# An encoder layer on one core: the mixer's TensorE work and loads in source order, probabilities turned one step later

## The chip, the cores and the metric

The kernel runs on one core of one Trainium2 chip. The metric is the device time of one execution in microseconds (us); lower is better. The engines are named as in the profile: PE (TensorE; PEld is its weight load), DVE (VectorE), ACT (ScalarE), POOL (GpSimd) and SP (SyncE). SP only issues DMA transfers; POOL issues a few on a queue of its own.

## The reference

One layer on x of 512 positions by 1024 channels, all in float32:

```python
x = x + 0.5 * swiglu(rms_norm(x, ffn1_norm), ffn1_w_gate, ffn1_w_up, ffn1_w_down)   # D_FF = 2752
h = rms_norm(x, mix_norm)
u = h @ w_in                                  # [ fourier 512 | q 8x64 | k 2x64 | v 2x64 ]
f_out = fourier_mixer(u[..., :512], fnet_w, fnet_b)   # real(fft2) per group of 128, then a 128x128 map
a_out = gqa_attention(q, k, v, q_norm, k_norm)        # per-head rms_norm, 2-D rotary, softmax, 4 q heads a kv head
x = x + jnp.concatenate([f_out, a_out], axis=-1) @ w_out
x = x + 0.5 * swiglu(rms_norm(x, ffn2_norm), ffn2_w_gate, ffn2_w_up, ffn2_w_down)
return rms_norm(x, final_norm)
```

## The kernel before

Everything is kept transposed: x is eight tiles of 128 channels by 512 positions (`x[0]` to `x[7]`). Each operand of a product is split into a high part and a low remainder, and `product` (L100 to L103) makes three products of them: high by high, high by low, low by high. So a weight tile that comes from memory is used in three steps: SP issues the load into one of three `raw` buffers (`raw_tile`, L87), ACT writes the high part into a ring slot (L96; for `f0` and `f1` DVE does, L94), and DVE writes the low part into another (`lows`, L72). There are six such slots for weights in the mixer, that is three pairs; a pair is free when the products of the tile before are done.

The kernel has three stages: FFN1, the mixer, FFN2. Both FFNs are built inside `in_order()`, which fixes the order of PE's and SP's instructions to that of the source:

```python
def in_order():
    return tc.manual_schedule(engines={mybir.EngineType.PE, mybir.EngineType.SP})
```

In the mixer, before the change, a scheduler of the build sets the order on all engines from a simulated timeline. The last products of FFN1 are called `dn` in the profile (its down projection).

The mixer begins with two memory pools; their tiles lie where FFN1's tiles were. `cos` and `sin` (L557, L559; 256 KB each) are loaded by SP into them, `chan`, `pos` (1 MB) and `odd` by POOL (L842). Then come, in the source's order:

- `project(c, name)` for k, q0, v, q1, q2, q3: a load `raw_in`, the split, and eight steps of `product` with 512 columns into one PSUM bank.
- `rope`: a square, the rotation with cos and sin. For q1, q2 and q3 (`SWAP_DMA`) ACT writes `own_q` (L587), and SP copies its four blocks of 32 partitions in another order to `sw_q` (four DMAs, L591); then DVE multiplies and adds (L596, L599, L600).
- `heads`: sums of squares per head with PE (`pq`, L607), then small DVE operations (L612 to L614, L618) and a power on POOL (L615).
- `keys`: a broadcast `kw` on DVE (L638) is turned by PE (`kp`, L644) and scales the keys, which are split into `ks`. `query` makes `qa` and `qb` (L627, L629). `value_stacks` turns the values (`vp`) into `vst`.

From there on two streams are woven together. `attend(n)` does for step n the scores of one pair of heads and one block of 128 queries (`s`, two products; then a maximum on DVE, L781, L782, and the exponential on ACT, L784, into `e`), the turn of an earlier step (`pt`, four transposes, L790; then ACT's copy `ph`, L793, and DVE's low part `pl`), and the values of a still earlier one (`o`, L809 and L810). A step's index counts 4 head pairs by 2 key heads by 4 blocks, 32 in all. `fill` is a list of the other work with a cost for each: the rest of q1 to q3, the Fourier projections (`f`, L700 to L702), their weight map (`map`), the transform over positions (`dft`) and over channels (`pc`, `psn`). Ahead of each step, entries of `fill` are run until their share of the total cost is reached, a tenth ahead (`FILL_LEAD`).

After the last step, w_out runs over eight output blocks d. Each sums eight parts k: 0 to 3 are the Fourier groups, 4 to 7 the head pairs; the bank is added to `x[d]`, and the norm of FFN2 begins.

Of the kernel before, what the change touches and what calls it, by code (L numbers as in the profile page):

```python
# [16 lines left out]
KD = D // P  # L17
# [7 lines left out]
FILL_LEAD = 0.1  # L25
# [18 lines left out]
def encoder(ctx, tc, A, out):  # L44
# [8 lines left out]
    def bank(name):  # L53
        return pp.tile([P, S], F32, tag="bank", name=name)
# [9 lines left out]
    def in_order():  # L64
        return tc.manual_schedule(engines={mybir.EngineType.PE, mybir.EngineType.SP})

    def run(steps):
        for _, f, a in steps:
            f(*a)

    def lows(lo, src, hi):
        nc.vector.tensor_tensor(out=lo, in0=src, in1=asf(hi), op=ALU.subtract)  # L72
# [17 lines left out]
    def weights(src, name, n=KD, raw=None):  # L90
        raw = raw or raw_tile(src, name, n)
        hi, lo = weight_slots()
        if name in HI_DVE:
            nc.vector.tensor_copy(hi[:, :n, :], raw[:, :n, :])  # L94
        else:
            nc.scalar.copy(hi[:, :n, :], raw[:, :n, :])  # L96
        lows(lo[:, :n, :], raw[:, :n, :], hi[:, :n, :])
        return hi, lo

    def product(ps, whi, wlo, mhi, mlo, first, last):  # L100
        nc.tensor.matmul(ps, whi, mhi, start=first, stop=False)  # L101
        nc.tensor.matmul(ps, whi, mlo, start=False, stop=False)  # L102
        nc.tensor.matmul(ps, wlo, mhi, start=False, stop=last)  # L103

    class Norm:
# [41 lines left out]
        def sum(self, ps, c, parts, first=True, last=True):  # L147
            for i, p in enumerate(parts):
                nc.tensor.matmul(
                    ps[:, 2 * c : 2 * c + 2], p[:, c * P : (c + 1) * P], ones,  # L150
                    start=first and i == 0, stop=last and i == len(parts) - 1,
                )
# [391 lines left out]


    n2 = Norm(2)
    with tc.tile_pool(name="mix", bufs=1) as mp, tc.tile_pool(name="mixt", bufs=1) as mt:

        more = mp.tile([P, 2, KD * P], F32R, name="more")
        more = [more[:, i, :] for i in range(2)]  # L550
# [167 lines left out]
        mh, ml = ([e[g // 2][g % 2].rearrange("p a b -> p (a b)") for g in range(4)] for e in (eh, el))  # L718
# [52 lines left out]
        def scores(t, b, c):  # L771
            if b == 0 and c == 0:
                zs[t] = tp.tile([P, 4, 2], F32, tag="z", bufs=2, name=f"z{t}")
            q = (qa, qb)[b][t]
            cs = slice(c * P, (c + 1) * P)
            ps = bank(f"s{t}{b}{c}")
            nc.tensor.matmul(ps, q[:, cs], kst[b][0], start=True, stop=False)
            nc.tensor.matmul(ps, q[:, cs], kst[b][1], start=False, stop=True)
            f = sc[:, c, 2 + 2 * t + b : 3 + 2 * t + b]
            mx = tp.tile([P, 1], F32, tag="mx", bufs=8, name=f"mx{t}{b}{c}")  # L780
            nc.vector.tensor_reduce(out=mx, in_=ps, axis=AX.X, op=ALU.max, negate=True)  # L781
            nc.vector.tensor_tensor(out=mx, in0=mx, in1=f, op=ALU.mult)  # L782
            e = temp(f"e{t}{b}{c}")
            nc.scalar.activation(e, ps, AF.Exp, bias=mx, scale=f, accum_out=zs[t][:, c, b : b + 1])  # L784
            prob[t, b, c] = e

        def turn(t, b, kc):
            pt = bank(f"pt{t}{b}{kc}")
            for c in range(4):
                nc.tensor.transpose(pt[:, c * P : (c + 1) * P], prob[t, b, c][:, kc * P : (kc + 1) * P], ident)  # L790
            ph = mt.tile([P, S], F32R, tag="ph", bufs=3, name=f"ph{t}{b}{kc}")
            pl = mt.tile([P, S], F32R, tag="pl", bufs=3, name=f"pl{t}{b}{kc}")
            nc.scalar.copy(ph, pt)  # L793
            lows(pl, pt, ph)
            parts[t, b, kc] = ph, pl
            if b == 1 and kc == 0:

                zw = tp.tile([P, 4, 2, HD], F32, tag="wide", bufs=1, name=f"zw{t}")
                nc.vector.reciprocal(zs[t], zs[t])
                nc.gpsimd.tensor_copy(zw, zs[t].unsqueeze(3).to_broadcast([P, 4, 2, HD]))  # L800
                zs[t] = zw

        def values(t, b, kc):
            if kc == 0:
                outs[t, b] = bank(f"o{t}{b}")
            po = outs[t, b]
            ph, pl = parts[t, b, kc]
            w = vst[:, b, kc].rearrange("p a e -> p (a e)")
            nc.tensor.matmul(po, w, ph, start=kc == 0, stop=False)  # L809
            nc.tensor.matmul(po, w, pl, start=False, stop=kc == 3)  # L810
            if kc == 3:
                own = slice(b * HD, (b + 1) * HD)
                if b == 0:
                    pair[t] = tp.tile([P, S], F32, tag="u", name=f"oo{t}")
                o = pair[t]
                nc.scalar.copy(o[own], po[HD:P])
                nc.vector.tensor_tensor(out=o[own], in0=po[0:HD], in1=o[own], op=ALU.add)
                if b == 1:
                    zp = bank(f"zp{t}")
                    for c in range(4):  # L820
                        nc.tensor.transpose(
                            zp[:, c * P : (c + 1) * P], zs[t][:, c].rearrange("p a b -> p (a b)"), ident
                        )
                    nc.vector.tensor_tensor(out=o, in0=zp, in1=o, op=ALU.mult)
                    nc.scalar.copy(qa[t], o)
                    lows(qb[t], o, qa[t])
# [31 lines left out]
        fill = []  # L858
# [34 lines left out]
        def attend(n):  # L893
            def at(m):
                return m // 8, m // 4 % 2, m % 4

            if n < 32:
                scores(*at(n))
            if 4 <= n < 36:
                turn(*at(n - 4))  # L900
            if n >= 6:
                values(*at(n - 6))

        whole = sum(c for c, _, _ in fill)
        done = 0.0
        for n in range(38):
            while fill and done < whole * (FILL_LEAD + (1 - FILL_LEAD) * n / 38):
                done += fill[0][0]
                run([fill.pop(0)])
            attend(n)  # L910
        run(fill)

        mh, ml = mh + [qa[t] for t in range(4)], ml + [qb[t] for t in range(4)]
        for d in range(KD):
            whi, wlo = weights(A["wo"][d], f"o{d}")
            ps = bank(f"out{d}")
            for k in range(KD):
                product(ps, whi[:, k, :], wlo[:, k, :], mh[k], ml[k], k == 0, k == KD - 1)
            nc.vector.tensor_tensor(out=x[d], in0=ps, in1=x[d], op=ALU.add)
            n2.add(d)  # L920

# [5 lines left out]
    ready = (3, 4, 5)  # L927
# [158 lines left out]
```

## Time and profile before

| | us |
|---|---|
| median of 3 runs | 882.02 (881.49 to 883.07) |
| the profiled execution, its own time | 882.0 |
| its span in the profile | 880.1 |
| PE busy | 863.1 |
| DVE busy | 640.4 |
| ACT busy | 451.0 |
| first product of the mixer (`k`) starts at | 353.17 |
| first product of w_out (`out`) starts at | 478.28 |

Times inside the span are counted from its start. A line of a group or of the timeline has the source line (L101), engine, operation, output and inputs by their names in the program, shape, count and duration; `SPq` is SP issuing a DMA. In a table by stage the columns are the stretch, its length, the busy time and count of PE, PEld, DVE, ACT and POOL, the granted clock of PE, the DMA engines' busy share and GB/s. "A <- B: t, n, m" in a list of waits says that A waited for B, t us in total, n times, m at the longest. A matmul's end is modelled, so from start to start is the measure of what one costs in a stream.

### The profile page before, as it was taken

The page shows a single profiled execution, that of the slowest core. Times are in us where ns is not written, and L with a number is a line of the kernel's source. Part 1 is how long each engine was busy: PE and PEld are TensorE (multiplying, and loading weights), DVE is VectorE, ACT ScalarE, POOL GpSimd, SP SyncE. Part 2 cuts the span into 40 slices and gives each one's busy share as a digit, 9 for nine tenths or more (in the row PEclk, how much of TensorE's full clock was granted, in tenths as well). Part 3 has the DMA queues.
Part 4 walks back from the last instruction along what each step waited for, and adds up shares of the span by engine and source line. Part 5 has one row for each costly group of instructions (what it writes and reads, how often), then busy time and mean ns, then how long its engine had stood idle before and what let it go on. Part 6 is the DMA issues. An engine that isn't in the chain of part 4 may idle for free.

```text
span 880.1 us, 13432 instructions
## 1 busy us (share of the span) xinstructions
PE 863.1 (98%) x5334; PEld 766.7 (87%) x5334; DVE 640.4 (73%) x1003; ACT 451.0 (51%) x746; POOL 24.7 (3%) x32
## 2 busy tenths in 40 slices
PE   8999999999999999999999999999999999999995
PEld 5888999889989988888888888889998999889985
DVE  7798788459757837699888558977975688469444
ACT  7454466226525634677775436535652365327432
POOL 0000000000000000211000000000000000000002
PEclk9999999999999999999999999999999999999998
DMA  7324232333243113521110223242224232322212
GB/s 245 112 67 164 98 118 86 99 116 104 69 141 114 55 36 108 204 83 37 50 48 25 94 67 127 75 141 97 108 79 140 88 119 69 105 110 85 73 36 96
DMA packets 29150, 85.55 MB, mean 97 GB/s; under 512 B 3488, under 2 KB 6560, under 8 KB 28960
## 3 DMA queue, kind: packets, MB, share of 16 engines
q1 hardware_dynamic: 28560, 83.37, 28.1%
q0 software_dynamic: 384, 1.32, 0.5%
q8 instruction: 41, 0.67, 0.3%
q14 instruction: 21, 0.17, 0.1%
q10 hardware_dynamic: 144, 0.02, 0.0%
HBM read 81.81 MB, written 2.10 MB: 95 GB/s over the span
## 4 chain that ended last, share of the span: by engine, by line
PE 56%; issue 39%; DVE 2%; ACT 2%; DMA 1%; POOL 0%; SPq 0%; POOLq 0%; ACTq 0%; DVEq 0%
PE r L304 10%; PE q L304 5%; PE dn L103 4%; PE dn L101 4%; PE dn L102 4%; PE p L304 3%; PE gu L103 2%; PE gu L102 2%; PE gu L101 2%; PE out L101 2%; PE out L103 2%; PE out L102 2%; PE pt L790 1%; PE q L101 1%; PE q L102 1%
## 5 line engine op out<-in xcount | busy, mean ns | idle before, releaser
L304 PE MATMUL r<-rt,ring 128*128 128x256 f32 x1584 | 207.2, 283 | 0.0
L304 PEld LDWEIGHTS r<-rt,ring 128*128 128x128 f32 x1584 | 196.1, 188 | 2.4
L101 PE MATMUL dn<-at,ring 128*128 128x512 f32 x324 | 128.0, 395 | 0.8 <-ACT ring L96 0.8
L103 PE MATMUL dn<-at,ring 128*128 128x512 f32 x324 | 127.9, 395 | 0.3 <-DVE ring L72 0.3
L102 PE MATMUL dn<-at,ring 128*128 128x512 f32 x324 | 127.9, 395 | 0.0
L390 DVE SCALAR_TENSOR_TENSOR xt<-dn,xt 128x512 f32<-128x512 f32 x62 | 42.8, 690 | 89.4 <-PE dn L103 89.4
L304 PE MATMUL q<-rt,ring 128*128 128x256 f32 x792 | 104.8, 282 | 0.0
L96 ACT CAST ring<-raw_dn 128x768 fp32r<-128x768 f32 (+3 forms) x64 | 48.1, 754 | 108.2 <-PE dn L102 89.8
L304 PEld LDWEIGHTS q<-rt,ring 128*128 128x128 f32 x792 | 98.7, 188 | 0.0
L72 DVE TENSOR_TENSOR ring<-s,ring 128x1024 fp32r<-128x1024 f32 x66 | 80.3, 1220 | 16.7 <-PE r L304 9.7
L265 ACT CAST ring<-s 128x1024 fp32r<-128x1024 f32 x66 | 69.3, 1050 | 37.4 <-PE r L304 19.2
L103 PEld LDWEIGHTS dn<-at,ring 128*128 128x128 f32 x324 | 61.0, 188 | 15.2 <-DVE ring L72 0.7
L101 PEld LDWEIGHTS dn<-at,ring 128*128 128x128 f32 x324 | 60.9, 188 | 14.8 <-ACT ring L96 1.0
L102 PEld LDWEIGHTS dn<-at,ring 128*128 128x128 f32 x324 | 60.9, 188 | 13.9
L72 DVE TENSOR_TENSOR ring<-raw_dn,ring 128x768 fp32r<-128x768 f32 (+3 forms) x64 | 54.5, 854 | 11.3 <-ACT ring L96 8.9
L304 PE MATMUL p<-rt,ring 128*128 128x256 f32 x396 | 52.4, 282 | 0.0
L72 DVE TENSOR_TENSOR ring<-raw_g,ring 128x1024 fp32r<-128x1024 f32 x33 | 40.4, 1223 | 15.5 <-PE p L304 10.9
L304 PEld LDWEIGHTS p<-rt,ring 128*128 128x128 f32 x396 | 49.3, 188 | 0.0
L265 ACT CAST ring<-raw_g 128x1024 fp32r<-128x1024 f32 x33 | 34.6, 1049 | 22.9 <-PE r L304 9.9
L101 PE MATMUL gu<-ring 128*128 128x512 f32 x112 | 44.1, 394 | 0.9 <-ACT ring L527 0.9
L102 PE MATMUL gu<-ring 128*128 128x512 f32 x112 | 43.9, 392 | 0.0
L103 PE MATMUL gu<-ring 128*128 128x512 f32 x104 | 41.1, 395 | 0.8 <-DVE ring L72 0.7
(308 smaller groups left out, 1514.0 us busy)
## 6 DMA issues: line engine op xcount, KB each, us to landing
raw_g<-in_wgu SPq DMA_DIRECT2D x33, 512.0 KB, 3.7
raw_u<-in_wgu SPq DMA_DIRECT2D x33, 512.0 KB, 4.3
raw_dn<-in_wd SPq DMA_DIRECT2D x40, 384.0 KB, 3.0
raw_gu<-in_wgu SPq DMA_DIRECT2D x16, 512.0 KB, 3.6
raw_o<-in_wo SPq DMA_DIRECT2D x8, 512.0 KB, 3.5
raw_in<-in_wins SPq DMA_DIRECT2D x6, 512.0 KB, 4.1
raw_dn<-in_wd SPq DMA_DIRECT2D x8, 320.0 KB, 2.9
raw_dn<-in_wd SPq DMA_DIRECT2D x8, 256.0 KB, 2.6
```

The costliest lines, as they stand in the source:

```text
L72: nc.vector.tensor_tensor(out=lo, in0=src, in1=asf(hi), op=ALU.subtract)
L96: nc.scalar.copy(hi[:, :n, :], raw[:, :n, :])
L101: nc.tensor.matmul(ps, whi, mhi, start=first, stop=False)
L102: nc.tensor.matmul(ps, whi, mlo, start=False, stop=False)
L103: nc.tensor.matmul(ps, wlo, mhi, start=False, stop=last)
L265: nc.scalar.copy(hi, src)
L304: nc.tensor.matmul(ps, a[:, ks], b[:, i], start=first and i == 0 and o == 0, stop=i == KH - 1 and o == 2, skip_group_check=not first,)
L390: nc.vector.scalar_tensor_tensor(out=x[d][:, t], in0=ps[:, t], scalar=0.5, in1=x[d][:, t], op0=ALU.mult, op1=ALU.add)
L790: nc.tensor.transpose(pt[:, c * P : (c + 1) * P], prob[t, b, c][:, kc * P : (kc + 1) * P], ident)
```

## The change

The mixer too is built inside `in_order()`. The probabilities of step n are turned at step n+5 (before: n+4) and multiplied with the values at step n+7 (before: n+6), so there are 39 steps. In w_out the parts are summed in the order 0, 1, 2, 4, 5, 6, 3, 7 (before: 0 to 7). No computation is added or left out.

```diff
-    with tc.tile_pool(name="mix", bufs=1) as mp, tc.tile_pool(name="mixt", bufs=1) as mt:
+    with in_order(), tc.tile_pool(name="mix", bufs=1) as mp, tc.tile_pool(name="mixt", bufs=1) as mt:
...
             if n < 32:
                 scores(*at(n))
-            if 4 <= n < 36:
-                turn(*at(n - 4))
-            if n >= 6:
-                values(*at(n - 6))
+            if 5 <= n < 37:
+                turn(*at(n - 5))
+            if n >= 7:
+                values(*at(n - 7))
 
         whole = sum(c for c, _, _ in fill)
         done = 0.0
-        for n in range(38):
-            while fill and done < whole * (FILL_LEAD + (1 - FILL_LEAD) * n / 38):
+        for n in range(39):
+            while fill and done < whole * (FILL_LEAD + (1 - FILL_LEAD) * n / 39):
...
+        ready = 0, 1, 2, 4, 5, 6, 3, 7
         for d in range(KD):
             whi, wlo = weights(A["wo"][d], f"o{d}")
             ps = bank(f"out{d}")
-            for k in range(KD):
-                product(ps, whi[:, k, :], wlo[:, k, :], mh[k], ml[k], k == 0, k == KD - 1)
+            for k in ready:
+                product(ps, whi[:, k, :], wlo[:, k, :], mh[k], ml[k], k == ready[0], k == ready[-1])
```

DVE, ACT and POOL stay with the scheduler. The source has the loads of cos and sin ahead of the first `project`.

## The prediction

> **What bounds the kernel now.** I read first the page's busy times and chain, then a table by stage of the mixer (353 to 527 us), then who waits for whom there, then SP's queue at the mixer's entrance, since SP's order is what the change rewrites.
>
> ```profile
> PE 863.1 (98%) x5334; PEld 766.7 (87%) x5334; DVE 640.4 (73%) x1003; ACT 451.0 (51%) x746; POOL 24.7 (3%) x32
> ```
>
> TensorE (PE) is the bound: 17 us without a product in 880.1. What it can gain in the mixer is its idle time there. The stage table (PE busy is the second number):
>
> ```profile
> 353.00:380.00 27.00, 27.00 (x138) 22.63 (x137) 19.76 (x34) 17.63 (x26) 5.82 (x6) 1.00 0.51 179
> 380.00:400.00 20.00, 20.00 (x106) 16.69 (x105) 19.20 (x41) 16.18 (x32) 2.78 (x2) 1.00 0.24 70
> 400.00:410.00 10.00, 8.75 (x59) 7.44 (x58) 9.87 (x24) 7.60 (x17) 2.24 (x2) 1.00 0.24 73
> ...
> 430.00:440.00 10.00, 9.09 (x66) 8.20 (x65) 8.00 (x17) 6.62 (x15) 0.00 (x0) 1.00 0.30 105
> ...
> 450.00:460.00 10.00, 9.51 (x61) 8.01 (x60) 8.92 (x17) 8.50 (x16) 0.00 (x0) 1.00 0.32 105
> 460.00:470.00 10.00, 9.60 (x65) 8.00 (x64) 8.81 (x19) 6.90 (x17) 0.23 (x1) 1.00 0.15 54
> 470.00:480.00 10.00, 9.54 (x64) 8.41 (x63) 8.82 (x20) 6.36 (x14) 0.39 (x1) 1.00 0.01 2
> 480.00:527.00 47.00, 47.00 (x205) 37.90 (x204) 26.70 (x37) 19.23 (x27) 0.00 (x0) 1.00 0.21 69
> ```
>
> PE is full up to 400 and in w_out. Idle shows in five rows: 1.25 + 0.91 + 0.49 + 0.40 + 0.46 = 3.5 us. The modelled tail of a product hides part of each stall; from start to start along PE's timeline, less the usual pitch (0.231 us for 512 columns, 0.119 for 256, 0.109 for a transpose), the loss from 353.2 to 478.3 is 5.7 us, 4.4 of it in five stalls (404, 437, 459, 466, 471). So 5.7 us is all that any order of the attention stage can bring. DVE is at 19.2 of 20 in the second row: it has no room there.
>
> Now the entrance. SP's timeline, SP's waits, and PE's timeline at the same time:
>
> ```profile
> 334.12 17.50 SPq L87 DMA_DIRECT2D raw_in<-in_wins  x4
> 353.36 0.33 SPq L557 DMA_DIRECT2D cos<-in_cos  x1
> 353.74 0.43 SPq L559 DMA_DIRECT2D sin<-in_sin  x1
> 355.52 1.46 SPq L87 DMA_DIRECT2D raw_in<-in_wins  x2
> ```
>
> ```profile
> SPq L557 <- PE dn L103: 1.7, 1, 1.7
> ```
>
> ```profile
> 352.94 0.39 PE L103 MATMUL dn<-at,ring 128*128 128x512 f32 x1
> 352.94 0.19 PEld L101 LDWEIGHTS k<-ring 128*128 128x128 f32 x1
> 353.17 0.40 PE L101 MATMUL k<-ring 128*128 128x512 f32 x1
> ```
>
> The first four weight tiles of the mixer are issued from 334.12 on, under FFN1's last products. The load of cos waits 1.7 us for a product of FFN1's `dn` (its tile lies in FFN1's memory) and goes out at 353.36, after the last one. PE passes from `dn` to `k` with no gap, because `k`'s weights are there.
>
> **The change, part by part.** The built program of the changed kernel has SP in source order: cos, sin, and only then raw_in 0, 1, 5, 2, 3. The wait ahead of cos is on the same product as before, the last of `dn`. So all weight loads of the mixer queue behind FFN1's end.
>
> *Opening.* cos at 353.36, sin at 353.74 (0.43), raw_in 0 at about 354.2. How long until it lands? The nearest rows:
>
> ```profile
> DMA to landing us min/median/max: 3.5/4.1/7.4
> ```
>
> ```profile
> q0 software_dynamic: 70, 0.57, 93.1%
> q1 hardware_dynamic: 7, 0.03, 4.8%
> ```
>
> The first is of the six raw_in loads: 3.5 to 4.1 on a quiet queue; the two issued at 355.5 and 356.7 took 7.3 and 7.4. The second pair is the DMA share by queue from 358 to 360: the 1 MB load of pos, which POOL issues at 354.24 on its own queue q0, has the engines nearly alone, and SP's q1 stands. raw_in 0 would be issued 1.3 us before those two, behind cos and sin, beside the same pos. Bounds: 4.1 (358.3) and the landing of the load whose place it takes (362.8); I take 361.9, next to the 7.3 row. Then the cast on ACT (1.05; the first product needs it), then the low part on DVE (1.23; the third product needs it), hops 0.15: third product of `k` at 364.3 instead of 353.63: **+10.7** (7.1 to 11.6). Nothing covers it, as PE too stands in source order and `k` is next.
>
> The Trainium skill ("DMA: Bandwidth & Descriptors", Queues, rings and completion order) says that each DMA engine takes turns between queues, packet by packet. By that rule raw_in 0 would get about half the engines and the opening would be about 1 us shorter; the 93% against 4.8% speak against it here, and the row decides.
>
> *Clock.* PE would stand 10 us, which it nowhere does in the trace of before. The nearest row is the start of the kernel, PE's only start from rest: 8 products of 512 columns in 3.56 us, 0.427 us from start to start, where later ones take 0.231. 8 x 0.196 = **+1.6** (0 to twice that). The Trainium skill ("TensorE: Matmul & The Clock Gate", Part 1) says that the array runs at half speed after some 3.4 us of rest, until some 3.4 us of work; an estimate by it is 1.7 us. The granted clock reads 1.00 in that first stretch, so that column will not show it.
>
> *Key transposes kp.* They now stand after 2 of v's 8 steps instead of after all of v. They need kw (L638). On DVE kw stands behind the low part of raw_in 3, which needs ACT's cast, which needs the end of q0's products (its ring slot). From q0's end: 1.05 + 1.23 + 0.16 (L618) + 0.43 (L638) + hops = 3.1; PE brings only rp (0.44) and 6 products (1.39) in between: **+1.3** (0 to 3).
>
> *raw_in 4 behind q1's swap.* Before, it went out at 356.7. Now SP issues it after the four sw_q1 copies, which wait for own_q1. From q1's end: square and own 1.4, four issues 2.5, landing 3.6 to 4.1: there at 7.8. ACT's order puts its cast behind qa1 and qb1, whose rotation needs sw_q1 landed (2.0 after issue, at 5.9), two DVE passes and a reduction (7.6), two casts (8.9): cast done at 10.0, low part, behind three DVE operations, at 12.05. PE is there at 8.7 (24 products of q2 5.5, five scores 2.3, pq 0.45, pt 0.44). It waits 1.35 for the cast and 1.6 more for the low part: **+3.0** (0 to 4). The later loads f0 to f3 pass the same way behind sw_q2 and sw_q3; f0 is due some 12 us after q3 begins and by the same count comes at the limit: in the next term.
>
> *Turn at n-5, values at n-7, 39 steps for 38.* The counts of products stay; a step is about 2.8 us, so score to turn and turn to values have two steps each at the tightest, where a reduction, exponential, cast and low part take 0.68 + 0.17 + 0.98 and 0.59 + 0.68. This should remove the stalls of before, **-5.7**, but a fixed order can't swap in other work when DVE is late; I leave **+2.0** for what remains (0 to 5.7).
>
> *w_out.* The head parts k = 3 and 7 come last: 18 products, 4.2 us, lie before them in the first block. PE already has no gap there (last table row), so 0.
>
> **Sum** against the profiled execution's own time 882.0 (span 880.1 and 1.9 around it; the median 882.02 is the same): 10.7 + 1.6 + 1.3 + 3.0 + 2.0 - 5.7 = +12.9, **894.9 us**. What follows the mixer is untouched and shifts whole.
>
> **Rivals.** (B) The opening costs what I say, but kp and raw_in 4 are ready in time and the attention stage runs without a stall: 10.7 + 1.6 - 5.7 = +6.6, 888.6. For: two more steps of slack. Against: the chains above run through DVE, 96% busy from 380 to 400.
> (C) Fixed order makes DVE or ACT the limit of the stage: before, transposes were split 3+1 and the two products of one score set apart, to let late operands pass. At 0.25 us a step, 32 steps are 8 instead of 2: 901.
> (D) Faster: the hold doesn't come, because the memory under cos is free before FFN1's end and SP goes on in time. Then without 10.7 and 1.6 the rest is +0.6, and with raw_in 4 also early -2.4: 879.6. It decides from the point where hold and the two new waits together stay under 5.7 - 2.0 = 3.7 us. Against: the 1.7 us wait on `dn`, and 353.36. Even the shortest landing, 3.5, makes the hold alone 6.5.
> That the change does less than it says is out: the built order shows PE and SP in source order.
>
> **How the numbers follow.** Forecast 0.66 (own range 891 to 899), B 0.15, C 0.16, D 0.03. The range takes in B and C's near half: 888.5 to 901. A measurement tells about 0.2% (1.8 us) from no change; D gives 0.02 faster and 0.01 within, the rest is slower.
>
> **What would show it.** SP's timeline with cos ahead of raw_in and the first raw_in at 354.2; PE idle for 9 to 11 us before `k`, released by ACT's cast and DVE's L72; `k`'s first products at a pitch near 0.43; PE waits at kp on DVE L638 and at q3's start on ACT L96 and DVE L72; fewer waits of `o` and `f` on ACT after 400. It is wrong if raw_in is issued before 353, if PE goes on from `dn` to `k` without a gap, or if idle after 400 grows past 6 us.

## The result and the profile after

The changed kernel takes 901.47 us (median of 5 runs, 899.2 to 901.98) where the kernel before takes 882.0: the ratio is 1.0213 (1.0201 to 1.0225), slower by 2.1%. The profiled execution is one of 899.34 us, with a span of 897.3. The five runs fall into two groups, 899.2 and 899.3, and 901.5 to 902.0; the last experiment looks for what parts them.

The page's busy times of the changed kernel:

```profile
PE 868.1 (97%) x5334; PEld 770.0 (86%) x5334; DVE 641.2 (71%) x1003; ACT 452.4 (50%) x746; POOL 25.8 (3%) x32
```

The same 5334 products, 29 us without one instead of 17, and 5 us more of busy time. The entrance first. SP's timeline:

```profile
354.00 0.33 SPq L557 DMA_DIRECT2D cos<-in_cos  x1
354.37 0.43 SPq L559 DMA_DIRECT2D sin<-in_sin  x1
354.90 12.30 SPq L87 DMA_DIRECT2D raw_in<-in_wins  x5
396.02 2.48 SPq L591 DMA_DIRECT2D sw_q<-own_q  x4
398.55 0.58 SPq L87 DMA_DIRECT2D raw_in<-in_wins  x1
...
419.86 2.41 SPq L591 DMA_DIRECT2D sw_q<-own_q  x4
422.37 1.02 SPq L87 DMA_DIRECT2D raw_f<-in_winf  x2
```

No weight tile of the mixer is issued before 354.90; before the change the first went out at 334.12. Further down, each weight load stands behind four `sw_q` copies. PE's timeline at the entrance (the bracket is the idle time and what ended it):

```profile
353.57 0.40 PE L103 MATMUL dn<-at,ring 128*128 128x512 f32 x1
364.22 0.80 PE L101 MATMUL k<-ring 128*128 128x512 f32 x1 [10.26 <-ACT ring L96]
364.82 0.63 PE L102 MATMUL k<-ring 128*128 128x512 f32 x1
```

PE stands 10.26 us where it had no gap, and `k` then runs slowly. The table by stage of the changed kernel shows that stretch and the later rows with idle time (PE busy is the second number, the granted clock the third from the end):

```profile
353.80:364.20 10.40, 0.16 (x1) 0.00 (x0) 2.05 (x3) 2.29 (x3) 1.68 (x3) 0.74 0.88 323
364.20:369.00 4.80, 4.74 (x10) 3.31 (x11) 3.68 (x3) 2.09 (x2) 0.00 (x0) 0.50 0.47 152
...
400.00:410.00 10.00, 8.67 (x43) 6.57 (x42) 9.15 (x20) 7.96 (x16) 1.64 (x1) 1.00 0.25 76
...
420.00:430.00 10.00, 7.14 (x48) 5.91 (x47) 9.06 (x21) 7.05 (x15) 2.60 (x1) 1.00 0.52 169
430.00:440.00 10.00, 10.00 (x75) 9.27 (x75) 9.34 (x22) 7.25 (x15) 2.25 (x2) 1.00 0.11 43
470.00:480.00 10.00, 8.98 (x56) 7.40 (x56) 9.97 (x18) 8.29 (x16) 0.00 (x0) 1.00 0.38 131
```

The granted clock is 0.50 for the first 4.8 us of `k`. The waits of PE from 350 to 520 name what ends each idle time:

```profile
PE k L101 <- ACT ring L96: 10.3, 1, 10.3
PE pt L790 <- ACT e L784: 2.9, 2, 2.8
PE q L103 <- DVE more L72: 1.2, 1, 1.2
PE kp L644 <- DVE kw L638: 0.9, 1, 0.9
PE dft L101 <- DVE pl L72: 0.9, 1, 0.9
```

Of the waits of before (`o` on `ph` 1.4 in two, `f` on `e` 1.3, `s` on `e` 0.5, `pt` on `e` 0.4) only `pt` on `e` is left, and it has grown to 2.8 in one piece, at 428; the others are new. That one is explained in ACT's timeline of the changed kernel:

```profile
426.18 1.04 ACT L96 CAST more<-raw_f 128x1024 fp32r<-128x1024 f32 x1 [1.12 <-DMA raw_f<-in_winf]
427.13 0.77 ACT L784 ACTIVATE e<-s,mx,sc 128x512 f32<-128x512 f32 x1
```

ACT waits for the weight tile that SP issued at 422.37, behind q3's swap copies; the exponential for which PE waits stands behind that cast.

Added up from start to start, less the usual pitch, PE loses 22.1 us from 352 to 500, where the kernel before loses 5.9: the gap at `k` 10.4, the slow start of `k` 2.5, `kp` 1.1, the second half of q3 (raw_in 4) 0.3 + 1.3, the 420s 3.4, the `dft` wait and its row 1.5, w_out's start 0.8, and small change. The difference, 16.2, and a `dn` that ends 0.6 later make 16.8 of the 17.2 us between the spans.

### The profile page after: what moved, and what is told of

It reads as the page before. It is cut to its first block, busy times and chain, and to the rows that moved or that the text cites. A ratio compares the mean times of both kernels' runs of the same rounds, so it can differ in the third digit from the quotient of the medians.

```text
span 897.3 us, 13422 instructions
## 1 busy us (share of the span) xinstructions
PE 868.1 (97%) x5334; PEld 770.0 (86%) x5334; DVE 641.2 (71%) x1003; ACT 452.4 (50%) x746; POOL 25.8 (3%) x32
## 4 chain that ended last, share of the span: by engine, by line
PE 53%; issue 38%; DVE 3%; DMA 2%; ACT 1%; SPq 1%; POOL 0%; POOLq 0%; ACTq 0%; DVEq 0%
PE r L304 10%; PE q L304 5%; PE dn L103 4%; PE dn L101 4%; PE dn L102 4%; PE gu L101 3%; PE p L304 3%; PE gu L102 3%; PE gu L103 3%; PE out L102 2%; PE out L103 2%; PE out L101 2%; PE pt L790 1%; DMA raw_in<-in_wins 1%; DVE ring L72 1%
## 5 line engine op out<-in xcount | busy, mean ns | idle before, releaser
L72 DVE TENSOR_TENSOR ring<-s,ring 128x1024 fp32r<-128x1024 f32 x66 | 80.3, 1221 | 17.3 <-PE r L304 10.3
L101 PE MATMUL gu<-ring 128*128 128x512 f32 x112 | 45.0, 401 | 0.7 <-ACT ring L527 0.7
L102 PE MATMUL gu<-ring 128*128 128x512 f32 x112 | 44.8, 400 | 0.0
L103 PE MATMUL gu<-ring 128*128 128x512 f32 x104 | 41.6, 400 | 0.0
```

## Experiments

**1. PE alone in order.** The later turn and the order of w_out's parts stay; SP goes back to the scheduler.

```diff
-    with in_order(), tc.tile_pool(name="mix", ...
+    with tc.manual_schedule(engines={mybir.EngineType.PE}), tc.tile_pool(name="mix", ...
```

> The changed kernel with only PE in source order in the mixer; SP's order is left to the scheduler, which puts raw_in ahead of cos and raw_f ahead of the swap copies. Theory (SP's order alone carries the loss): opening, raw_in 4 and the stall at 428 go, 13 + 1.7 + 2.9 = 17.6 us: about 881 to 883 us, as fast as before or a little faster. Rival (PE's fixed order costs by itself): 886 us or more, with new stalls on ACT and DVE after 380.

Measured: 879.89 us (879.37 to 881.0), ratio 0.9979 (0.9969 to 0.9989). SP issues raw_in from 333.92 on, as before the change, and PE's waits are `kp` 0.9, `dft` 0.9, `out` 0.3 and `pt` 0.2. So SP's order, and not PE's, carries the loss: taking it out alone brings 901.47 to 879.89, 21.6 us, more than the whole difference.

**2. SP alone in order, on the kernel before.** The converse: the lag of before, and PE with the scheduler.

```diff
-    with tc.tile_pool(name="mix", ...
+    with tc.manual_schedule(engines={mybir.EngineType.SP}), tc.tile_pool(name="mix", ...
```

> The kernel before, with SP alone in the source's order in the mixer (lag 4/6, parts 0 to 7, all other engines with the scheduler). Theory (the loss of the change is SP's order: loads behind cos and sin at the entrance, later loads behind the swap copies): raw_in 0 is issued at about 354.9, PE stands about 10 us at the entrance (the scheduler may find nothing else, as nothing of the mixer has weights), half clock after it, and PE is late again where raw_in 4 and the raw_f loads stand behind the copies: 893 to 900. Rival (SP's order hurts only together with PE's fixed order; with PE free, other work fills the gaps): at most 886.

Measured: 900.13 (896.77 to 902.16), ratio 1.0203 (1.0183 to 1.0222), just above the theory's upper end. The two longest waits of PE in this kernel:

```profile
PE k L101 <- ACT ring L96: 7.0, 1, 7.0
PE o L810 <- DVE pl L72: 4.0, 1, 4.0
```

With PE's order free, nothing else fills the entrance. The second wait looks like another form of the stall at 428 (argued from the timeline, not tested apart): raw_f goes out at 403.83 behind swap copies, its cast and low parts fall into a stretch where DVE is busy 9.87 of 10 us, and the values wait. The rival, that PE's order is needed for the harm, falls.

**3. The first loads ahead of cos and sin.** In the changed kernel the DMAs of cos and sin move behind raw_in 0, 1 and 5.

```diff
-        nc.sync.dma_start(out=cos, in_=A["cos"])
-        nc.sync.dma_start(out=sin, in_=A["sin"])
...
         q0 = project(1, "q0")
+        raw5 = raw_tile(A["wins"][5], "in5")
+        nc.sync.dma_start(out=cos, in_=A["cos"])
+        nc.sync.dma_start(out=sin, in_=A["sin"])
...
-        val = project(5, "v")
+        val = project(5, "v", raw=raw5)
```

> The changed kernel with one edit: the loads of cos and sin stand in the source behind raw_in 0, 1 and 5 instead of ahead of them; PE and SP stay in source order. Theory (the opening is most of the loss): PE goes from dn to k without a gap and at full pitch, so the 10.4 us gap and the 2.5 us at half pitch go: about 886 to 888 us, with the stalls at kp (1.1), raw_in 4 (1.7), and the transposes at 428 (2.9) still there. Rival (the loss comes from the fixed order in the attention stage, and the gap at the opening was only a place where it shows): 895 us or more.

Measured: 889.04 (888.97 to 892.76), ratio 1.009 (1.007 to 1.011). `k` follows `dn` with no gap, which is worth 12.4 us: the entrance was as large as 10.4 + 2.5. The time is a little above what was expected: the raw_f stall stays, now at 414, and half clock follows it. raw_in 2, here the first weight tile behind cos and sin, landed 4.9 us after its issue, in time for PE. The longest wait of PE, and the row of that stretch:

```profile
PE pt L788 <- ACT e L782: 3.1, 2, 2.9
```

```profile
410.00:420.00 10.00, 7.07 (x36) 6.51 (x36) 7.13 (x17) 6.17 (x13) 1.21 (x2) 0.70 0.55 181
```

**4. The later loads ahead of the swap copies.** raw_in 4 and the first three raw_f are issued some products before the `rope` whose copies held them; cos and sin stay first.

```diff
+                for i in {(1, 2): ["in4"], (2, 2): [0], (2, 5): [1], (3, 5): [2]}.get((t, k), ()):
+                    add(fetch, i)
```

> The changed kernel with raw_in 4 and raw_f 0, 1, 2 issued by SP ahead of the swap copies sw_q1, sw_q2, sw_q3 instead of behind them; cos and sin still first. Theory: the stalls at raw_in 4 (1.7 us) and at 428 (2.9 us, ACT's cast of raw_f 2 in front of the exponential) go, the opening stays: 899.3 - 4.6 = 894 to 895.5 us; and since the runs near 902 are taken to be those in which the stall at 428 puts PE's clock at half a second time, all runs fall in one group. Rival (the 428 stall is DVE and ACT being full, not a load): 898 us or more, in two groups.

Measured: 895.12 (893.91 to 898.09), ratio 1.0156 (1.0135 to 1.0177). The wait for raw_in 4 is gone, and so is the stall at 428, which stood in the turn of step 8. A shorter one has come in the turn of step 4, where PE waits for an exponential that itself waits for a maximum on DVE (a line of ACT's timeline, then one of PE's):

```profile
411.49 0.78 ACT L784 ACTIVATE e<-s,mx,sc 128x512 f32<-128x512 f32 x1 [1.60 <-DVE mx L782]
412.41 0.33 PE L790 MATMUL pt<-ident,e 128*128 128x128 f32 x1 [1.68 <-ACT e L784]
```

So the stall of 2.9 came from the late load, as it went with it. In its place DVE, which now has the early raw_f to split at that time, sets a smaller one. That the time lies in the expected range is in part luck: the theory had the opening stay, but in the profile the gap at `k` is only 7.2, as raw_in 0 landed 5.1 us after its issue instead of 8.15, with the same loads around it. That is about half of the 6.3 us gained. The runs spread from 893.9 to 898.1, so the one group that was expected did not come either.

**5. Both load edits.**

> The changed kernel with both moves of loads: cos and sin behind raw_in 0, 1 and 5, and raw_in 4 and raw_f 0, 1, 2 ahead of the swap copies; PE and SP in source order. Theory (where loads stand in SP's queue is all of the loss): the same as with SP left to the scheduler, 879.5 to 881.5 us. Rival (SP in source order costs something else too): 883 us or more.

Measured: 888.82 (its runs spread from 883.78 to 890.93), ratio 1.0062 (1.004 to 1.0083): a miss. The edits don't add up to a free entrance. As in experiment 3, SP's queue has raw_in 2 behind cos and sin, beside the load of pos, but in this profile it lands 8.6 us after its issue, where it took 4.9 there. ACT's timeline shows where that is paid:

```profile
363.03 1.04 ACT L96 CAST ring<-raw_in 128x1024 fp32r<-128x1024 f32 x1 [6.61 <-DMA raw_in<-in_wins]
363.98 0.59 ACT L581 ACTIVATE sq_k<-k 128x512 f32<-128x512 f32 x1
```

ACT's order puts the cast of that tile ahead of the square of `k`, so `k`'s sums (1.4) and the key transposes (3.5) wait for a load that they don't use. The scheduler's order of SP has four raw_in ahead of cos and sin, this one three; it is that fourth tile that comes late. Why it is late here and was not in experiment 3 is not shown: one difference is raw_in 4, which now goes out right behind raw_in 2 and 3. So the rival, a further cost of SP in source order, holds as far as a tile behind cos and sin can land late; whether that explains all nine runs is open, as only one of them was traced.

**6. The lag under a fixed PE order.** The kernel of experiment 1 with turn and values at n-4 and n-6, and the changed kernel with the same.

```diff
-            if 5 <= n < 37:
-                turn(*at(n - 5))
-            if n >= 7:
-                values(*at(n - 7))
+            if 4 <= n < 36:
+                turn(*at(n - 4))
+            if n >= 6:
+                values(*at(n - 6))
```

> PE alone in source order (SP left to the scheduler), with the turn at n-4 and the values at n-6 again. Tells what the extra step of lag is worth where no load is late. Theory (the lag covers the latency from score to turn): stalls of the transposes on the exponential come back, 883 to 888 us against 879.9 with the lag. Rival (lag matters only when loads are late): 880 to 881 us.

> The changed kernel with the turn at n-4 and the values at n-6 again, 38 steps; the rest as changed. Theory (the extra step covers the latency from score to turn): the stall at 428 grows from 2.9 to some 5 us and others come, 1 to 5 us slower than the changed kernel, 901 to 906 us. Rival (the lag does nothing, loads set the stalls): within 1 us of the changed kernel.

Measured: 887.16 (885.3 to 887.54) and 907.7 (905.51 to 908.4), so 7.3 and 6.2 us more than with the later turn; the second lies above its expected range. In the first, five waits of `pt` for `e` make 4.8 us, against 0.2 in experiment 1, and a half clock of 3.4 us follows two of them. In the second, six such waits make 7.1 us against 2.9 in the changed kernel, and half clock follows them twice, for 10.24 and 3.41 us; the profiled run of the changed kernel has none there. Under a fixed order the later turn is what keeps PE busy.

**7. No fixed order, only the later turn,** with w_out's parts as changed and as before.

```diff
-    with in_order(), tc.tile_pool(name="mix", ...
+    with tc.tile_pool(name="mix", ...
```

```diff
-        ready = 0, 1, 2, 4, 5, 6, 3, 7
+        ready = tuple(range(KD))
```

> The changed kernel without the fixed order in the mixer: only the lag of 5 and 7 steps and the order of the parts in w_out are changed, the scheduler orders all engines. Theory (the fixed order of PE is what removes the stalls of before): within 1 us of the kernel before, 881 to 883 us. Rival (the lag alone removes them): 879 to 880.5 us.

> No fixed order in the mixer, turn at n-5 and values at n-7, but w_out's parts in the order 0 to 7. Theory (the later turn alone brings the gain of the version without a fixed order): 878 to 879.5, the ratio within 0.001 of that version. Rival (the parts' order matters, as the last heads' values come late for w_out's first block): 880 to 881.5, with a wait of out at the first block.

Measured: 878.42 (878.05 to 878.52), ratio 0.9961 (0.9946 to 0.9975), and 878.62 (877.81 to 880.01), ratio 0.9963 (0.9949 to 0.9976). These beat both kernels, and the parts' order is worth nothing that can be told. The only wait of PE in the mixer of the first:

```profile
PE dft L101 <- DVE oo L817: 0.8, 1, 0.8
```

The loss from 352 to 500 is 2.4 us, 3.5 less than before the change; the time is 3.4 less than the kernel before took beside it (881.82). So the later turn brings the gain by itself. In medians the change comes apart as: later turn -3.4 (878.62), parts -0.2, PE's order +1.5 (879.89), SP's order +21.6 (901.47).

**8. Is it the rest or the load that costs at `k`?** 46 unused products of 512 columns between `dn` and `k`, to keep PE at work.

```diff
+        warm = bank("warm")
+        for i in range(46):
+            nc.tensor.matmul(warm, hh[0][:, 0:P], hh[0], start=True, stop=True)
         key = project(0, "k")
```

> The changed kernel with 46 products of 512 columns between dn and k that nothing uses, into a PSUM bank of their own; they fill the wait for raw_in 0 (46 x 0.231 = 10.6 us). Theory (the half pitch after the wait, and its length that varies from run to run, are the clock's answer to PE's rest): k starts when it did, but at 0.231 from the first product; 896.5 to 897.5 us in every run, and the two groups of times, 899.3 and 901.9, become one. Rival (the slow start of k is a wait for operands): 899 to 902 us still, in two groups.

Measured: 900.02 (897.63 to 903.33): a miss. Seven of the products slipped in among `dn`, which ended 0.9 later, and the rest ended 1.3 us before `k`'s weights were there. The clock dropped again, for 3.41 us in place of 10.24, right behind the stretch that held this rest of 1.3 and one of 0.5, and a second time, for 3.41 us at 431.29, behind the stall at `pt`. The runs still lie in two groups. Less rest gave a shorter drop, which is what the theory says of the cause; that the slow start can be removed in this way is not shown.

**9. Is it pos that holds raw_in 0?** POOL's load of pos waits for a later value.

```diff
+        nc.gpsimd.tensor_copy(pos[:, 0, 0, 0:4], n1.r)
```

> The changed kernel, with the load of pos (1 MB, POOL's queue) held until FFN1's norm factor for the mixer (n1.r) is made, by a copy of four of its columns into pos ahead of its load. Theory (pos takes about half the DMA engines from raw_in 0, so that it lands 8.15 us after its issue): raw_in 0 lands 4 to 5.5 us after its issue, the gap at the first k is 6.3 to 8 us in place of 10.3, and the time is 895 to 898. Rival (the landing is long because five loads of raw_in share the queue, pos or not): the same gap, 899 to 902.

Measured: 898.74 (897.09 to 899.32), ratio 1.0188 (1.0174 to 1.0201). The gap at `k` is 6.65 and raw_in 0 lands 4.5 us after its issue, as the theory had it, and the time is just above its range, as half clock follows the stall at `pt` in the profiled run. But experiments 2 and 4 had landings of 4.9 and 5.1 us beside pos. That it can land soon in spite of pos is shown; that pos is why it landed late in the changed kernel isn't. Left open.

**10. The changed kernel once more.**

> The changed kernel once more. Its runs lie in two groups, 899.3 and 901.9. Theory (the second group has a second stretch at half clock after the 2.9 us stall near 428): a run near 899.3 has one stretch near 359, a run near 902 has a second one that begins 426 to 432. Rival: the profile of a run near 902 has the same one stretch, and the 2.5 us lie elsewhere.

Measured: 903.32. The table by stage, to be held against the rows of 420 and 430 above:

```profile
420.00:430.00 10.00, 7.08 (x43) 5.74 (x42) 9.17 (x21) 6.89 (x15) 2.60 (x1) 0.94 0.51 158
430.00:440.00 10.00, 10.00 (x58) 9.30 (x57) 6.51 (x15) 5.31 (x12) 1.64 (x1) 0.72 0.15 52
```

The stall is the same 2.85 us, but behind it the granted clock is 0.72 where it was 1.00, and PE does 58 instructions instead of 75. The trace's clock records give a second stretch at half clock from 428.74, 6.83 us long, which is 3.4 us of work lost; the first is 13.65 long instead of 10.24 and ends 6.6 instead of 4.9 us into `k`, another 0.8. Together 4.2, against 4.0 between the two profiled runs, so the theory held for this run. That the same parts the five runs above is likely, though only one of them was traced: the mean granted clock of a whole run is 0.989 and 0.988 in the two faster, 0.986, 0.984 and 0.984 in the three slower, and 0.984 in this one.

## Why the prediction was right in direction, and where its steps were off

It said 894.9, with 891 to 899 as the forecast's own range and 888.5 to 901 in all. The median is 901.47, half a microsecond above the wide range, and the profiled execution that the sum can be held against is 899.34. Slower, for the cause it named, but 4.4 us too little; that the sum comes this near owes something to errors that cancel, as the list shows.

- **Opening, +10.7 (7.1 to 11.6).** Right: 10.4 from start to start in the changed kernel. As a wait it is 10.3 there, 9.8 and 10.5 in two more profiles with the same entrance, and 7.0 and 7.2 where raw_in 0 landed in 4.9 and 5.1 us. The lower bound was met, the upper one was not reached.
- **The queue rule beside it.** The row that was to decide, q0 93.1% and q1 4.8%, did not carry over. The DMA share by queue from 358 to 360 in the changed kernel:

```profile
q0 software_dynamic: 58, 0.45, 58.4%
q1 hardware_dynamic: 99, 0.35, 45.3%
```

 With three weight tiles at hand q1 gets nearly half, as the Trainium skill ("DMA: Bandwidth & Descriptors", Queues, rings and completion order) has it: engines take turns between queues, packet by packet. Yet the landing was 8.15 us, not a microsecond less: the three tiles land 8.1 to 9.9 after issue, so q1's half seems to have gone to all three. In experiments 2 and 4 the first landed after 4.9 and 5.1 us and the other two after 8.1 to 8.9, so it need not go that way. The number was right on a wrong reason, and with some luck.
- **Clock, +1.6.** The mechanism was right, the size low: 2.5. Half clock did not end after the 3.56 us of the kernel's start but 4.9 us into `k`, so 10 products at 0.427 lose 2.0; the first three stand 0.60 to 0.66 apart, which makes the other 0.5 and wasn't explained. "That column will not show it" was wrong: the column reads 0.50. It read 1.00 at the kernel's start because the trace of before has no clock record ahead of 4.62 us.
- **`kp`, +1.3; raw_in 4, +3.0.** 1.1 and 1.65. The low part waits 1.3 as counted (1.6), the cast 0.3 instead of 1.35.
- **What remains, +2.0 (0 to 5.7).** Here the sum failed: 5.7 us from 420 to 500. The prediction saw that f0 to f3 pass behind the swap copies, put them "at the limit", and gave them nothing of their own. Half of the term, 2.9, is that one load, as its stall went when the load was moved (experiment 4), and it is not paid where it lands: ACT's order puts its cast ahead of an exponential. And a stall of that length can set off the clock a second time, 3.4 us in the runs of the slower group; the prediction had the clock at the entrance alone.
- **-5.7 for the stalls of before.** The old stalls are gone (430 to 470 has 0.1 us of loss), but not for nothing: with SP's order taken out again, 1.9 us of the 5.7 reach the time under a fixed PE order (`kp`, `dft` and `out` still wait) and 3.4 without one. The gain is the later turn's, not the fixed order's, as experiments 6 and 7 show.
- **w_out, 0.** Right within 0.5 (a wait of `out` for `el`).
- **Rivals.** C's number, 901, is near the result, but not by its mechanism: PE is full, 10.00 of 10, from 430 to 470, and no step costs more. B fell on `kp`, raw_in 4 and raw_f, D on the hold.

Of the 4.4 us, what remains is 3.7 over, opening and clock 0.6, and `dn` ended 0.6 later in this run; `kp` and raw_in 4 are 1.5 under; some 1 us lies in gaps too small to be named.

## What to carry to other kernels

A fixed order for the queue that issues loads is a promise about every wait in it: a DMA that waits for memory of the stage before, or for an intermediate, holds each weight tile behind it, so put loads without such a wait first, or leave that queue to the scheduler. The distance between producing and using (here one step more) was worth 3.4 us by itself and, without the fixed order, cost no time that the runs show. A stall on PE of 2 us or more, or two shorter ones close together, is to be counted with the clock that can follow it.

## What the runs showed of the hardware

In the traces' clock records, half clock comes in pieces of 3.41 us (3.41, 6.83, 10.24, 13.65) whose borders lie on one grid within a run. The table counts, in a piece at full clock, PE's time without a product (ends as modelled) and the columns of the products in it (512 for a product of 512 columns; one at a border is shared out at 0.231 us for 512):

| run | piece | idle in it | columns | half clock behind it |
|---|---|---|---|---|
| experiment 8, behind the stall at `pt` | 427.87 to 431.29 | 1.19 | 2695 | 3.41 |
| both load edits | 368.09 to 371.50 | 1.80 | 2986 | none |
| changed kernel | 423.70 to 427.11 | 1.83 | 2734 | none |
| experiment 8, at `k` | 363.02 to 366.43 | 1.84 | 2550 | 3.41 |
| changed, lag 4 and 6 | 422.95 to 426.37 | 2.07 | 1758 | 10.24 |
| PE alone, lag 4 and 6 | 466.69 to 470.10 | 2.10 | 2037 | 3.41 |
| pos later | 420.38 to 423.80 | 2.25 | 1855 | 6.83 |
| loads first | 410.63 to 414.04 | 2.41 | 1495 | 6.83 |
| changed kernel again | 425.33 to 428.74 | 2.70 | 881 | 6.83 |

So a stall of 2.8 us sets it off or not by how it falls on the grid: in the changed kernel's profiled run it was cut in two, 1.83 and 0.94, in the other 2.70 lay in one piece. Idle time alone does not part the pieces: the clock dropped behind one with 1.19 us idle and not behind one with 1.83. The columns do. Of all pieces at full clock in the 14 traces of this case, the 28 with 2,695 columns or fewer were followed by half clock, the 3,524 with 2,952 or more were not, and two with 2,734 went one each way; at 0.231 us for 512 a piece holds some 7,560. Products of few columns fill PE's time without counting for much: in the first row eight `pq` of 2 columns each take 0.95 us. The Trainium skill ("TensorE: Matmul & The Clock Gate", Part 1) tells of a free-running activity window of 4096 cycles and of half rate after an idle window of about 3.4 us; the piece's length agrees, but here a piece at little over a third of the usual columns was enough.

In the six profiles with all raw_in behind cos and sin and the load of pos beside them (the changed kernel twice, experiments 2, 4 and 8, and the lag of 4 and 6), raw_in 0, 512 KB, landed 4.9, 5.1, 7.7, 8.1, 8.15 and 8.35 us after its issue. What decides between the two ends wasn't found.
